# A planned single-core decoder trunk: sample keys earlier, sample state later, other weight buffers, another estimate of transfers

## The chip, the cores and the metric

The kernel runs on one core of one Trainium2 chip. The metric is the device time of one execution in microseconds (us); less is better. TensorE (PE) multiplies, with its weight loads (PEld) as a row of their own; VectorE is DVE, ScalarE is ACT, GpSimd is POOL, and SyncE (SP) issues all DMAs of this kernel from one queue. TensorE writes to PSUM; the other tiles lie in SBUF. Where this text says bank, it means a PSUM tile of 128 x 512 fp32.

## The reference, cut to what matters

One inference step of a hybrid decoder trunk (one layer). There are two groups of tokens: a **prompt** of 512 new tokens, and a **sample** group of 8 running sequences with one new token each, which bring a recurrent state and 256 useful rows of cached keys and values per sequence.

```
h = x @ w_in                                   # 1024 -> 3600
qa, ka, va, za, ga, qb, kb, vb, gb = split(h)
mixer A (4 heads): S_t = diag(a_t) S_{t-1} + k_t^T v_t;  o_t = q_t S_t     # gated linear attention
mixer B (8 heads): dilated sliding-window attention with a relative-position bias
mix = concat(o_a * silu(ga), o_b * silu(gb))
y   = mix @ w_out
x_new = layer_norm(sqrt(sqrt(2)) * x + y) * ln_g + ln_b     # alpha = 2 ** 0.25
```

Outputs are x_new for both groups, the recurrent state of both groups after the step, and the new rows of keys and values. For the sample group the state update is elementwise: state (8 sequences x 4 heads x 64 x 128, 1 MB) times a decay, plus the outer product of the new key with the new value.

## The kernel before, in words

**Dense work.** The projections are done in groups of 128 or 256 columns of w_in: ka, qa, qb, kb, vb, gb, va, ga, in this order, then w_out. A 32-bit product is made of three products of a high and a low part, so each weight tile is loaded raw (512 KB, buffers with the tag `r`, of which there are 2), copied to a high part by ACT (`hi_...`) and subtracted to a low part by DVE (`lo_...`); the two parts take buffers with the tag `w` (6) or others named below. A dense matmul has 128 weights and 256 or 264 columns. `feature` (L626) makes one group of 128 columns: two banks (u = 0 and 1, half of the tokens each), 24 matmuls for each bank, then an evacuation by another engine. `gates` (L685) calls it for the four groups of ga and of gb; their evacuation takes sigmoid steps on ACT (`sg`) and a product on DVE. The output product has two parts, `out_first` (banks `ps_yf`, transposed back as `ps_yt`) and `out_unit` (banks `ps_y`); after them come layer norm and the stores of the rows, in `norm` (L1593).

**The order is planned, not written.** All of this is made of generators (tasks), added with a priority (a low number is urgent): `add(sample_state(), 47)` (L1636), the dense chain with 100. While the program is built, a planner (`Plan`, L195) takes the next instruction again and again: of all tasks that can go on, the one whose instruction would start first by the planner's own estimate of time, ties by priority. Each engine's queue then runs in the order in which the planner emitted it; nothing is reordered on the chip. So a changed estimate in `Op` (L82) or in `issue` (L344) moves instructions on all engines. The estimate of a DMA is a rate from the shape of its rows (L105), a constant `LATE` (L76) if the queue is still busy, and a factor for DMAs that start early (L361). `At(mark, n)` holds a task until n marks of that name were emitted; `Need(tag, ...)` takes a buffer or bank from a pool and holds the task until one is free. The pools are `SLOTS` (L63: `g` 24, `w` 6, `r` 2, `sv` 5, `pt` 4, ...) and `BANKS` (L72: `d` 3, `s` 3, `t` 2). All instructions that the planner emits carry the line L366 in the profile, the one line that calls the engine; they are told apart by their tiles.

**All DMAs are issued by SP, in order.** A DMA whose buffer is not yet free holds all later ones. Eight semaphores are used in turn, so that a DMA also waits for the one that was issued eight places before it.

**The sample group**, which runs beside the prompt's dense work:
- `sample_queries` (L1209): the query rows (`q_rows`) go to a scratch row in memory (`qsd`), are broadcast back for each sequence (`qbc`, 256 KB) and multiplied on POOL with the sequence's cached keys (`past`, 512 KB, tag `sv`), four products of 128 x 256 for each of 8 sequences; DVE reduces them into `lt`.
- `sample_softmax` (L1229) turns the logits by TensorE (`ps_sl`), takes the softmax and stores it to scratch (`psd_s`). `sample_values` (L1282) broadcasts it back (`pb`, two DMAs of 256 KB for each sequence), loads cached values (`vv`, 512 KB, tag `sv`), multiplies on POOL and reduces on DVE (`o_pv`).
- `sample_state` (L1345): for each of two halves a load of the state (`s`, 512 KB), two broadcasts of the new values (`v`, 256 KB each), then eight products on ACT and eight multiply-adds on DVE of 128 x 128, and the store of the half. Its tiles have the tag `sv`, and its end sets the mark `sample`, as the end of `sample_softmax` does.

**Attention of the prompt.** For each head and query tile, scores come by `ps_s`; DVE adds a strip of bias (`strip<-tabr`, 128 KB or 256 KB, read from a table in scratch) and makes `pr`; ACT and DVE normalize it by the sums `ms`; TensorE transposes it (`ps_pt`), and ACT or DVE evacuates that as `pt`.

**Weights' buffers.** `Group.part` (L482) takes a buffer for a high or low part: tag `w`, and for w_out alone also `sv` (once the mark `sample` stands at 2, which is when `sample_softmax` and `sample_state` are both through), `pt` (once the mark `ob1` stands at 4) and `g`. `first_loads` (L546) issues the first loads in a fixed order, constants (`cf`, `rb_raw`, `cm_w`, `gn`, `ct_raw`) among them, ahead of the weights' own task. `residual` (L1483) loads the rows of x that are added to the output product (`y`, 512 KB); for the third and fourth of four tiles it waits for the mark `y0_done` at 4.

## Time and profile before

| what | value |
|---|---|
| median of 3 runs | 285.9 us (285.61 to 286.2) |
| profiled execution | 285.7 us, its span 283.9 us |
| mean granted TensorE clock | 0.992 |
| HBM read, written | 46.24 MB, 6.03 MB |

The span reaches from the first to the last recorded instruction or transfer; 1.8 us of the profiled execution lie around it. The views used below are the page (busy time of each engine, slices, chain that ended last), windows (busy time of each engine in a stretch), waits (what ended an engine's idle time), the chain in order of time (start, length, what), and groups by line and tile. Busy time of PE is modelled: a matmul is shown longer than the time until the next one starts, so that back-to-back matmuls overlap in the record.

### The profile page before, as it was taken

What the parts mean: (1) busy time and instruction counts of PE and PEld (TensorE: products, weight loads), DVE (VectorE), ACT (ScalarE), POOL (GpSimd) and SP (SyncE); (2) the same over time, 40 slices, a digit from 0 to 9 for tenths busy, and PEclk for the clock granted to TensorE, in tenths of its full rate; (3) what the DMA queues carried; (4) which work ended last, traced back from release to release, by engine and by line L of the source; (5) the groups of instructions that cost most, each with busy time, mean ns of one, the idle gap of its engine ahead of it and who ended that gap; (6) DMA issues with size and microseconds to landing.
All of it is one profiled execution on the core that took longest, in us unless ns stands there. A gap on an engine that the chain in (4) does not pass through costs nothing.

```text
span 283.9 us, 7064 instructions
## 1 busy us (share of the span) xinstructions
PE 272.5 (96%) x2760; PEld 253.3 (89%) x2760; DVE 208.4 (73%) x499; ACT 157.8 (56%) x450; POOL 54.5 (19%) x72
## 2 busy tenths in 40 slices
PE   8999999999999999999999899999999999999990
PEld 5899999998999999988989899999999999997880
DVE  3846797997969976579778896336679797439855
ACT  5738654543655755378868663426589886213201
POOL 4000000000295039300034354443000000000000
PEclk9999999999999999999999999999999999999996
DMA  6965622276874698747999999988455994872311
GB/s 197 290 179 174 182 76 76 76 204 156 302 207 141 175 279 254 205 150 227 233 209 199 214 231 234 221 215 182 121 166 160 260 284 146 209 138 111 131 76 74
DMA packets 59945, 52.27 MB, mean 184 GB/s; under 512 B 12507, under 2 KB 50693, under 8 KB 59911
## 3 DMA queue, kind: packets, MB, share of 16 engines
q1 hardware_dynamic: 59802, 51.73, 68.9%
q8 instruction: 22, 0.36, 0.5%
q14 instruction: 13, 0.10, 0.1%
q10 hardware_dynamic: 108, 0.07, 0.1%
HBM read 46.24 MB, written 6.03 MB: 184 GB/s over the span
## 4 chain that ended last, share of the span: by engine, by line
PE 72%; DMA 12%; DVE 8%; ACT 4%; issue 2%; SPq 1%; DVEq 0%; ACTq 0%
PE ps_qb L366 8%; PE ps_y L366 8%; PE ps_yf L366 7%; DMA strip<-tabr 7%; PE ps_gb L366 5%; PE ps_qa L366 4%; PE ps_vb_f L366 4%; PE ps_va_f L366 4%; PE ps_va L366 4%; PE ps_vb L366 4%; PE ps_ga L366 4%; PE ps_kb L366 3%; PE ps_ka L366 3%; DMA s<-in_state_dram 3%; DMA x_raw<-in_xT_dram 2%; PE ps_pt L366 2%
## 5 line engine op out<-in xcount | busy, mean ns | idle before, releaser
L366 POOL TENSOR_TENSOR past<-past,qbc 128x256 f32<-128x256 f32 x32 | 25.3, 825 | 90.5 <-DMA past<-in_ck_dram 88.6
L366 POOL TENSOR_TENSOR vv<-vv,pb 128x256 f32<-128x256 f32 x32 | 26.0, 844 | 48.9 <-DVE gb L366 24.4
L366 ACT ACTIVATE pr<-pr,ms 128x128 f32<-128x128 f32 (+3 forms) x45 | 24.4, 549 | 14.9 <-DVE ms L366 14.8
L366 DVE CUSTOM_DVE_ANT_0 pr<-ps_s,strip 128x128 f32<-128x128 f32 (+3 forms) x32 | 14.4, 481 | 3.3 <-DMA strip<-tabr 2.0
L366 PE MATMUL ps_pt<-cf,pr 128*128 128x128 f32 x80 | 14.0, 276 | 0.3 <-DVE pr L366 0.2
L366 ACT ACTIVATE sg<-sg 128x264 f32<-128x264 f32 (+1 forms) x32 | 13.9, 433 | 0.3
L366 PE MATMUL ps_ka<-xx,hi_ka 128*128 128x264 f32 (+1 forms) x64 | 13.2, 303 | 0.7 <-DVE xx L366 0.7
L366 ACT COPY pt<-ps_pt 128x256 f32<-128x256 f32 (+3 forms) x27 | 11.4, 431 | 4.3 <-PE ps_pt L366 4.1
L366 PEld LDWEIGHTS ps_ka<-xx,hi_ka 128*128 128x128 f32 x64 | 10.8, 201 | 1.7 <-DVE xx L366 1.1
L366 DVE TENSOR_REDUCE o_pv<-vv 128x4 f32<-128x1024 f32 x8 | 9.7, 1214 | 1.6 <-POOL vv L366 1.6
L366 PEld LDWEIGHTS ps_pt<-cf,pr 128*128 128x128 f32 x80 | 9.4, 140 | 1.4 <-issue 0.5
L366 DVE TENSOR_SCALAR pr<-pr,ms 128x512 f32<-128x512 f32 (+3 forms) x19 | 10.0, 528 | 0.4
L366 ACT ACTIVATE rstd<-mv 128x1 f32<-128x1 f32 x4 | 0.7, 203 | 16.6 <-DVE mv L366 16.6
L366 ACT COPY feat_y<-ps_yf 128x256 f32<-128x256 f32 x8 | 3.0, 373 | 12.0 <-PE ps_yf L366 12.0
L366 PE MATMUL ps_pv<-pt,v 128*64 128x256 f32 (+1 forms) x96 | 9.5, 348 | 0.0
L366 DVE TENSOR_REDUCE lt<-past 128x16 f32<-128x1024 f32 x8 | 9.5, 1201 | 0.0
L366 PE MATMUL ps_ka<-xx,lo_ka 128*128 128x264 f32 (+1 forms) x32 | 9.3, 290 | 0.0
L366 PEld LDWEIGHTS ps_pv<-pt,v 128*64 128x64 f32 x96 | 6.3, 137 | 2.9
L366 DVE TENSOR_TENSOR xx<-x_raw,xx 128x520 fp32r<-128x520 f32 (+2 forms) x9 | 5.7, 640 | 4.1 <-ACT xx L366 4.1
L366 ACT ACTIVATE d<-d 128x512 f32<-128x512 f32 x11 | 6.8, 644 | 3.4 <-DVE d L366 3.4
L366 PE MATMUL ps_s<-kp,qh 64*128 64x128 f32 (+3 forms) x64 | 8.4, 345 | 0.0
L366 DVE COPY_PREDICATED near<-cm,ps_l 128x256 f32<-128x256 uint8 x12 | 6.1, 541 | 2.3 <-PE ps_l L366 2.3
(532 smaller groups left out, 1031.6 us busy)
## 6 DMA issues: line engine op xcount, KB each, us to landing
past<-in_ck_dram SPq DMA_DIRECT2D x8, 512.0 KB
vv<-in_cv_dram SPq DMA_DIRECT2D x8, 512.0 KB
pb<-psd_s SPq DMA_DIRECT2D x16, 256.0 KB
s<-in_state_dram SPq DMA_DIRECT2D x4, 512.0 KB
qbc<-qsd SPq DMA_DIRECT2D x8, 256.0 KB
strip<-tabr SPq DMA_DIRECT2D x8, 256.0 KB
y<-in_xp_dram SPq DMA_DIRECT2D x4, 512.0 KB
x_raw<-in_xT_dram SPq DMA_DIRECT2D x7, 260.0 KB
```

What stands on the lines that cost most here:

```text
L366: getattr(eng.eng, op.fn)(*op.args, **op.kw)
```

## The change

Seven edits; the arithmetic is the same.

1. **Estimate of transfers.** `LATE` 600 becomes 1600, the table of rates is another, and the factor 0.8 for early DMAs is gone. The planner's order follows from these numbers.
2. **Buffers for weights.** Once `ob1` stands at 4, every weight group (not only w_out) may take `pt` buffers, and `sv` buffers once `sample_softmax` is through (mark `sample` at 1, since `sample_state` sets it no more); `g` stays for w_out.
3. **First loads.** The constants become a task `constant_loads` that starts after the first raw weight load was emitted.
4. **`feature` is cut into halves**; for ga, groups 0 and 1 are made together (half u = 0 of both, then u = 1 of both), then groups 2 and 3.
5. **Sample's keys.** The first three key loads are emitted once the first group of qb is under way, not behind the query rows.
6. **Sample's state.** The task waits for the mark `y3` too, takes `g` buffers, emits the loads of both halves before any product, has priority 16.5 instead of 47, and sets no mark.
7. **`residual`** waits for `y0_done` at 1 instead of 4.

```diff
-LATE = 600.0
+LATE = 1600.0
...
-            rate = 60 if run <= 128 else 175 if x.ap[0][1] <= 64 else 340 if run >= 4096 else 230
+            rate = 150 if run <= 128 else 225 if x.ap[0][1] <= 64 else 320 if run >= 2048 else 290 if run >= 1024 else 262
             self.xfer = max(4 * total(x) / rate, 200)
-            self.late = 600 * (rate == 175)
+            self.late = 600 * (rate == 225)
...
-            self.dma = max(self.dma, start + 1300) + op.xfer * (1.0 if start < 2700 else .8 if start < 9000 else 1)
+            self.dma = max(self.dma, start + 1300) + op.xfer
...
             tags = ("w",)
-            if self.src is w_out:
-
-                tags += ("sv",) * (plan.marks["sample"] == 2) + ("pt",) * (plan.marks["ob1"] == 4) + ("g",)
+            if plan.marks["ob1"] == 4:
+
+                tags += ("sv",) * (plan.marks["sample"] == 1) + ("pt",) + ("g",) * (self.src is w_out)
...
         yield D.dma_start(zw[:, :, :16], za)
         mark("zw")
+        add(weight_loads(), 3)
+        add(constant_loads(), 3.5)
+
+    def constant_loads():
+        yield At("raw", 1)
         yield D.dma_start(cf, c_f[:, :C_E2])
-        add(weight_loads(), 3)
...
+        for u in range(2):
+            yield from half(g, evac, u)
+        g.done(0)
+
+    def half(g, evac, u):
         yield At(g.name)
-        for u in range(2):
-            ps = yield bank("d", f"ps_{g.name}{u}")
-            for k in range(KT):
-                yield from three(ps[:, :TW[u]], k, halves(k, u, g))
-            add(evac(ps, u), 2)
-        g.done(0)
+        ps = yield bank("d", f"ps_{g.name}{u}")
+        for k in range(KT):
+            yield from three(ps[:, :TW[u]], k, halves(k, u, g))
+        add(evac(ps, u), 2)
...
-        for i in range(4):
-            yield from feature(groups[f"{n}{i}"], gate_into(n, own, i))
+        for i in ((0, 1), (2, 3)) if n == "ga" else ((0,), (1,), (2,), (3,)):
+            for u in range(2):
+                for j in i:
+                    yield from half(groups[f"{n}{j}"], gate_into(n, own, j), u)
+            for j in i:
+                groups[f"{n}{j}"].done(0)
...
     def sample_queries():
+        def keys(bi):
+            past.append((yield Need("sv", f"past{bi}", [P, 2, 512])))
+            yield D.dma_start(past[bi], ck[bi])
+
+        past = []
+        yield At("qb", 1)
+        for bi in range(3):
+            yield from keys(bi)
         yield At("qb", 8)
...
-            past = yield Need("sv", f"past{bi}", [P, 2, 512])
-            yield D.dma_start(past, ck[bi])
-            add(sample_logit(bi, past, qbc), 50)
+            if bi > 2:
+                yield from keys(bi)
+            add(sample_logit(bi, past[bi], qbc), 50)
...
     def sample_state():
         yield At("vat_out")
+        yield At("y3")
+        sv = []
         for i in range(2):
-            s4 = yield Need("sv", f"s5{i}", [P, 4, 2, P])
+            s4 = yield Need("g", f"s5{i}", [P, 4, 2, P])
...
-            v4 = yield Need("sv", f"v4{i}", [P, 4, 2, P])
+            v4 = yield Need("g", f"v4{i}", [P, 4, 2, P])
...
+            sv.append((s4, v4))
+        for i, (s4, v4) in enumerate(sv):
             for bb in range(4):
...
-        mark("sample")
...
         if t in (2, 3):
-            yield At("y0_done", 4)
+            yield At("y0_done", 1)
...
-    add(sample_state(), 47)
+    add(sample_state(), 16.5)
```

## The prediction

> **What bounds the kernel now.** I read the page first, for the busy shares and the chain that ended last.

> ```profile
> PE 272.5 (96%) x2760; PEld 253.3 (89%) x2760; DVE 208.4 (73%) x499; ACT 157.8 (56%) x450; POOL 54.5 (19%) x72
> ...
> PE 72%; DMA 12%; DVE 8%; ACT 4%; issue 2%; SPq 1%; DVEq 0%; ACTq 0%
> ...
> L366 PE MATMUL ps_ka<-xx,lo_ka 128*128 128x264 f32 (+1 forms) x32 | 9.3, 290 | 0.0
> ```

> TensorE is the bound: every other engine has a quarter of the span or more to spare, and the rest of the chain is made of places where PE waited. The change leaves the number of dense matmuls alone, so it can save only PE's idle time. Windows of ten to fifty us show where that lies (window, its length, then busy us of PE, PEld, DVE, ACT and POOL).

> ```profile
> 0.00:10.00 10.00, 8.12 (x35) 5.46 (x36) 4.92 (x13) 5.71 (x10) 3.18 (x8) 1.00 0.77 238
> ...
> 60.00:80.00 20.00, 19.30 (x294) 17.75 (x295) 17.61 (x41) 10.34 (x29) 4.03 (x5) 1.00 0.77 226
> ...
> 90.00:100.00 10.00, 9.95 (x86) 9.47 (x86) 9.76 (x28) 6.51 (x23) 0.99 (x1) 1.00 0.60 176
> 150.00:160.00 10.00, 9.36 (x76) 8.42 (x75) 8.49 (x20) 7.07 (x20) 3.38 (x4) 1.00 0.99 208
> 160.00:170.00 10.00, 9.75 (x83) 9.21 (x85) 9.61 (x21) 7.89 (x20) 6.93 (x8) 1.00 0.99 225
> 220.00:230.00 10.00, 9.80 (x139) 9.39 (x136) 7.77 (x28) 8.92 (x39) 0.00 (x0) 1.00 1.06 262
> 240.00:250.00 10.00, 9.82 (x82) 9.60 (x81) 5.58 (x17) 2.22 (x7) 0.00 (x0) 1.00 0.86 198
> 270.00:284.00 14.00, 6.39 (x52) 6.04 (x50) 7.05 (x14) 1.40 (x6) 0.00 (x0) 0.83 0.19 76
> ```

> All other windows show PE full. Between 10 and 270 us PE is idle for 0.70 + 0.05 + 0.64 + 0.25 + 0.20 + 0.18 = 2.02 us; the rest is the start (1.88) and the end (7.61). A dense matmul starts every 0.12 us (the row of x84 below: 10.27 / 84) and is shown with 0.29 us (the row of `lo_ka`), so each stop costs 0.17 us more than its idle time. With eight stops (three in 60 to 80, two in 150 to 170, one in each of the others) that is 2.0 + 1.4, about 3.4 us: **the most that the middle can give back**. The waits of PE and the chain name the causes.

> ```profile
> PE ps_gb L366 <- DVE ms L366: 0.9, 1, 0.9
> PE ps_ka L366 <- DVE xx L366: 0.7, 2, 0.3
> PE ps_l L366 <- issue: 0.4, 1, 0.4
> PE ps_pt L366 <- DVE pr L366: 0.2, 1, 0.2
> PE ps_yf L366 <- DVE ga L366: 0.2, 1, 0.2
> PE ps_yf L366 <- DVE lo_wo__3663 L366: 0.2, 1, 0.2
> ```

> ```profile
> 22.93 10.27 PE ps_qa L366 x84
> ...
> 142.09 15.15 DMA strip<-tabr
> ...
> 158.56 1.13 DVE o_pv L366
> ...
> 160.25 1.81 PE ps_gb L366 x13
> ```

> The largest stop is at 160 us: gb's next bank is freed by a DVE product that stands behind the last head's softmax, and this waited for a bias strip that took 15.15 us from issue to landing.

> **The change, part by part.** (a) *Keys early, and the sample's chain.* POOL waits for keys from the start:

> ```profile
> POOL past L366 <- DMA past<-in_ck_dram: 88.6, 4, 72.3
> ```

> ```profile
> 36.00:58.00 22.00, 22.00 (x406) 21.62 (x406) 20.10 (x38) 11.35 (x22) 0.00 (x0) 1.00 0.27 74
> 120.00:128.00 8.00, 8.00 (x71) 6.83 (x68) 6.02 (x20) 5.81 (x16) 0.00 (x0) 1.00 0.41 133
> 128.00:157.00 29.00, 29.00 (x244) 25.92 (x243) 22.92 (x61) 22.88 (x56) 6.48 (x8) 1.00 0.99 218
> ```

> In the new order three key loads (3 x 512 KB) stand right behind the first load of kb, so they run in the stretch from 36 us with the DMA engines at 0.27, and cost nothing there: at 218 GB/s (the row of 128 to 157) they take 7 us of 22 that are three quarters free. They are no longer among the strips and query broadcasts around 70 us, so POOL can start at about 71 instead of 76 us (72.3 of wait behind its first work). Its remaining waits for keys, 88.6 - 72.3 = 16.3 us, shrink; I estimate that the last key product comes 6 to 8 us earlier. All that hangs on it moves alike: the sample's softmax, its store, and the 8 value loads and 16 broadcasts that fill the stretch from 128 us at 0.99. They start while the engines are at 0.41 (120 to 128). The strip issued at about 141 us then has some 8 us less queue ahead of it. It needs to land only 1.2 us sooner for the stop to vanish: idle 0.64 + 0.25, and twice 0.17 hidden, **-1.2 us**. The next thing late there would be DVE's `o_pv` behind POOL's values, which move forward with the chain.

> (b) *60 to 100 us.* Idle 0.75 and four stops' 0.17, 1.4 in all. The 0.4 of "issue" with its 0.17 is PE's own and stays. The others are waits for DVE, which is 88% busy in 60 to 80 and 98% in 90 to 100 us. The strips land sooner without keys beside them, but POOL now works beside DVE from 71 us. I bound it between all of it gone (-0.8) and the opposite (+0.8), and take **-0.3**. The same product shows why I don't take more: a low part of 128 x 1024 on DVE, without POOL and beside it.

> ```profile
> L366 DVE TENSOR_TENSOR lo_kb__982<-raw_kb__768,hi_kb__981 128x1024 fp32r<-128x1024 f32 x1 | 1.2, 1225 | 0.1
> L366 DVE TENSOR_TENSOR lo_kb__1198<-raw_kb__926,hi_kb__1197 128x1024 fp32r<-128x1024 f32 x1 | 1.8, 1766 | 0.0
> ```

> It grew by 0.54 us. [...]

> (c) *State late.* Sixteen multiply-adds on DVE and as many products on ACT leave the stretch of 207 to 238 us, as do 2 MB of loads and broadcasts and 1 MB of stores.

> ```profile
> L366 DVE SCALAR_TENSOR_TENSOR s<-v,ka_s,s x16: 341/344/352, 208.2 to 237.7; 128x128 f32<-128x128 f32 x16
> L366 ACT ACTIVATE s<-s,a_s x15: 385/394/470, 207.7 to 237.2; 128x128 f32<-128x128 f32 x15
> ```

> That frees 16 x 0.344 = 5.5 us on DVE and 16 x 0.394 = 6.3 us on ACT. With it the last w_out weights, which waited for `r` and other buffers, are split earlier (in the new order all their splits stand ahead of the mixing of A's output), so the stop of 240 to 250 goes: 0.18 + 0.17, **-0.35**. The stop of 220 to 230 (0.20 + 0.17) is a bank held until DVE evacuates a gate; it has less in front of it, but interleaved gates put the last evacuation as close to the bank's next use as before. I take half, **-0.18**; bounds -0.37 and +0.4.

> Where the work goes: behind `y3`, between the output's evacuations. DVE waits there today.

> ```profile
> DVE lt L366 <- ACT feat_y L366: 7.1, 3, 3.1
> DVE y L366 <- PE ps_y L366: 3.3, 2, 1.9
> DVE y L366 <- PE ps_yt L366: 1.9, 2, 1.5
> ```

> In the new order the first half's eight multiply-adds (2.75 us) and four of the second stand ahead of the row tiles, into waits of 7.1 + 1.9 us; the last four (1.4 us) go among the layer norm, with 3.3 us of waiting for PE left. So **0** at the end, with one condition: the vectors must have landed (first rival). ACT has 1.40 us of work in the last 14.

> (d) *Gates by halves, more buffers, constants as a task, residual at 1.* Two of ga's groups alternate by bank; each bank still takes 24 matmuls, 2.9 us, and its evacuation has two other banks' time, so 0; without that cover a bank waits for an evacuation as in the 0.20 row. More buffers let `va` and `ga` weights be split earlier: 0, as PE waits for none of them today. The constants behind the first weight load: the start's waits are for x (0.7, `xx`), whose loads come first in both orders: 0, bounds -0.3 and +0.3. The two `y` loads come earlier, in front of nothing that PE waits for: 0.

> (e) *The new order itself.* Some forty of the joints between PE and other engines have moved, by up to forty-five dense matmuls, when the two orders are laid side by side. Each may be a new stop, none of which the trace of before can show. Bounds: 0, and two stops of the size of the largest today, 2 x (0.9 + 0.17) = 2.1. I take one like the `issue` row, **+0.4**, since the six that exist are mostly this size.

> Sum: -1.2 - 0.3 - 0.35 - 0.18 + 0.4 = -1.6 us, on the profiled 285.7 (span 283.9 and 1.8 around it): 284.1. The profiled execution lies 0.2 below the median of 285.9, so 284.3 by the median.

> The end itself stays: after the last matmul comes a chain of one tile's layer norm and its store.

> ```profile
> 262.66 13.74 PE ps_y L366 x82
> 276.42 0.43 DVE y L366
> ```

> From 276.42 to the span's end of 283.9 it is 7.5 us that the diff doesn't touch.

> **The rivals.** *The state comes too late (slower).* DVE runs in order, so from the first multiply-add of the second half on, all row tiles stand behind that half's vectors. Their broadcasts are issued behind eight stores of key rows, each of which waits for the landing of an earlier DMA, and the load of the second half waits for A's output (`mla`) to be mixed, which TensorE first takes at 234.9 us. The rows say when these things are wanted, and what the state's own load can take:

> ```profile
> L366 PE MATMUL ps_yf<-mla,hi_wo__3249 x8: 282/286/287, 234.9 to 240.1; 128*128 128x264 f32 x8
> ```

> ```profile
> L366 DVE SCALAR_TENSOR_TENSOR y<-y,ps_yt x8: 403/415/422, 240.1 to 255.8; 128x256 f32<-128x256 f32 x8
> ```

> ```profile
> 219.31 7.24 DMA s<-in_state_dram
> ```

> If load and broadcasts each took 7.24 us with the stores between, from 236 on, the vectors would land near 251 us; DVE wants them some 2 us (four multiply-adds and more) ahead of the last `y` additions, which run up to 255.8 and will come 1.6 sooner, so at about 252: nothing. If the broadcasts took as long as the strip's 15.15 us, they would land near 259 us, DVE would stand for some 6.5 us, of which 3.3 are covered by its waits for PE: +3.2, so 284.3 + 3.2, about 287.5. It decides from a landing at about 255 us. Against it: DMA share after 236 us is moderate (0.86 in 240 to 250, with the stores). [...]

> *POOL in DVE's way (no change or slightly slower).* Some five two-input DVE operations more run beside POOL between 71 and 90 us; at up to 0.54 us each DVE is 2.7 us later, and a stretch where DVE is nearly full passes up to 1.6 on: the -0.3 becomes +1.3, and the total 285.9.

> *The strip is late all the same (the change doesn't do what it says).* If the planner puts other loads, of va's weights and values, ahead of that strip, the 15.15 us stay and the -1.2 is lost: 284.3 + 1.2 = 285.5.

> **How the numbers follow.** The forecast (a gain of 0.6 to 3) 0.56; the strip late 0.12 (half of it faster, half within); POOL in the way 0.12 (a third each); the state too late, or several new stops of (e) together, 0.20 (slower). A measurement of this kernel can tell about 0.2% (0.6 us) from no change. So faster 0.56 + 0.06 + 0.04 = 0.66, within 0.06 + 0.04 = 0.10, slower 0.04 + 0.20 = 0.24. The range: below, all that the middle has goes but issue's 0.57, -2.8, and the start's -0.3 with it, so 282.8; above, 287.0, which leaves out about one in ten, a state later than 257 us.

> **What would show it.** In the profile after: POOL's first key product near 71 us; a strip that lands before 156 us and no PE wait on `ms` near 160; PE full in 240 to 250; DVE's `s` products at 245 to 262 with no wait on `v<-vad`; the last `y` evacuation some 1.5 us earlier and 7.5 us from the end. Wrong would be: PE idle between 10 and 270 us still near 2 us but at other places (e), or DVE idle before `s` near 250 us and the row tiles late.

## The result, and the profile after

The changed kernel took **289.8 us** (median of 4 executions, 289.27 to 290.6) beside 286.05 (285.61 to 286.42) of the kernel before: ratio **1.0147 [1.0104, 1.019]**, slower, where 284.3 was forecast with a range to 287.0. The profiled execution is 289.65 us with a span of 287.9, so 4.0 us more span than before. Two later comparisons of the same two kernels gave 1.0009 and 1.006 (e9 and e13 below, on two chips); all further ratios are to the kernel before on the same chip, with a 95% interval. Medians and ratios leave out executions in a slower state of the chip, from which the profiles of e6, e8, e9, e10 and e12 come, so those spans are not compared.

The page of after, busy times and the shares of the chain that ended last:

```profile
PE 272.4 (95%) x2760; PEld 253.3 (88%) x2760; DVE 207.2 (72%) x500; ACT 157.3 (55%) x449; POOL 59.9 (21%) x72
...
PE 69%; DMA 13%; DVE 12%; issue 2%; ACT 2%; SPq 0%; DVEq 0%; ACTq 0%
```

PE has the same 2760 matmuls and the same busy time (272.5 before). All of the loss is therefore PE's idle time. The windows of after that answer to those of before (window, length, busy us of PE, PEld, DVE, ACT, POOL, then clock, DMA share, GB/s):

```profile
60.00:70.00 10.00, 8.30 (x202) 7.72 (x201) 6.73 (x12) 2.92 (x5) 0.00 (x0) 1.00 0.57 156
70.00:80.00 10.00, 9.39 (x81) 8.88 (x82) 9.17 (x23) 5.82 (x19) 7.75 (x8) 1.00 0.29 92
80.00:90.00 10.00, 9.88 (x90) 9.16 (x89) 8.21 (x25) 7.42 (x26) 5.95 (x9) 1.00 0.74 217
...
110.00:120.00 10.00, 8.02 (x65) 7.04 (x64) 5.57 (x9) 4.41 (x12) 5.06 (x4) 1.00 0.36 104
...
160.00:170.00 10.00, 8.40 (x70) 8.05 (x69) 9.96 (x23) 7.18 (x19) 3.56 (x5) 1.00 0.64 177
...
220.00:230.00 10.00, 10.00 (x164) 9.63 (x157) 6.54 (x22) 8.62 (x37) 0.00 (x0) 1.00 0.62 184
...
240.00:250.00 10.00, 10.00 (x85) 10.00 (x84) 4.51 (x17) 3.92 (x12) 0.00 (x0) 1.00 0.96 213
```

Between 10 and 270 us PE is now idle for 1.70 + 0.61 + 0.12 + 1.98 + 1.60 = 6.01 us, where it was 2.02: 4.0 more, which is the whole difference of the spans (the start is the same, and the end differs by 0.1). The stops of before at 220 to 230 and 240 to 250 are gone; three others have come or grown, at 65, at 113 and in 160 to 170 us. PE's waits in after name what ended each (us in total, times, longest):

```profile
PE ps_l L366 <- issue: 1.7, 1, 1.7
PE ps_pt L366 <- DVE pt L366: 1.6, 1, 1.6
PE ps_pt L366 <- DVE pr L366: 1.6, 2, 0.9
...
PE ps_pt L366 <- ACT pr L366: 0.6, 1, 0.6
PE ps_vb_f L366 <- DVE lo_vb__1796 L366: 0.4, 1, 0.4
```

The chain of after in order of time (start, length, what):

```profile
62.11 1.80 PE ps_l L366 x113
63.91 1.70 issue
65.61 0.49 PE ps_l L366 x15
...
104.20 8.24 DMA sel<-in_c_f_dram
112.67 0.28 DVE pt L366
113.00 0.33 PE ps_pt L366
...
115.15 0.68 DVE lo_vb__1796 L366
...
145.80 13.93 DMA strip<-tabr
...
169.26 0.41 DVE pr L366
...
280.34 0.43 DVE y L366
```

**113 us.** `sel` is a table of 56 KB that `sample_softmax` loads when it needs it; it took 8.24 us from issue to landing. DVE's timeline shows who stood behind it (start, length, operation, in brackets the wait before it):

```profile
106.58 1.20 DVE L366 TENSOR_REDUCE lt<-past 128x16 f32<-128x1024 f32 x1
...
112.53 0.21 DVE L366 TENSOR_TENSOR l<-ln_new,sel 32x64 f32<-32x64 f32 x1 [4.76 <-DMA sel<-in_c_f_dram]
112.67 0.27 DVE L366 COPY pt<-ps_pt 128x128 f32<-128x128 f32 x1
```

DVE ran in order: a product of 0.21 us that the sample wants held the evacuation of `pt`, which TensorE wanted and whose bank `ps_pt` had been written by 109.74 us, and the split `lo_vb__1796` (PE's 0.4) behind it. In the kernel before the same load is issued even later, at 105.9 us, but the product stands behind the evacuations of `pt` in DVE's queue and starts at 114.8; PE lost nothing there. DVE's timeline of before:

```profile
111.48 0.41 DVE L366 COPY pt<-ps_pt 128x256 f32<-128x256 f32 x1
...
114.83 0.21 DVE L366 TENSOR_TENSOR l<-ln_new,sel 32x64 f32<-32x64 f32 x1 [0.20 <-DMA sel<-in_c_f_dram]
```

**65 us.** The stop is called `issue`: PE waited for nothing that the profile shows. It cuts the third batch of 128 small matmuls `ps_l`, after 113 of them here and after 109 in before, with 1.70 us here and 0.41 there. The chain of before:

```profile
62.75 1.75 PE ps_l L366 x109
64.50 0.41 issue
64.90 0.54 PE ps_l L366 x19
```

The page's list of queues has one of the kind `instruction`:

```profile
q8 instruction: 22, 0.36, 0.5%
```

(packets, MB, share). In the trace of after, a block of 16 KB on it began 0.88 us after the start of that batch, in before 0.19 us ahead of it. What sets its time is the question of the second group of runs (there: the instruction block).

**160 to 170 us.** The strip lands at 145.80 + 13.93 = 159.73 us (157.24 before), and the splits and `o_pv` products that waited with it fill DVE for 9.96 of the next 10 us, ahead of the `pr` that PE waits for.

**The end.** From the last `ps_y` evacuation at 280.34 us to the end of the span are 7.6 us, against 7.5.

### The profile page after: what moved, and what is told of

Read it like the earlier page. It is cut to its first block, busy times and chain, and to the rows that moved or that the text cites. A ratio compares the mean times of both kernels' runs of the same rounds, so it can differ in the third digit from the quotient of the medians.

```text
span 287.9 us, 7062 instructions
## 1 busy us (share of the span) xinstructions
PE 272.4 (95%) x2760; PEld 253.3 (88%) x2760; DVE 207.2 (72%) x500; ACT 157.3 (55%) x449; POOL 59.9 (21%) x72
## 4 chain that ended last, share of the span: by engine, by line
PE 69%; DMA 13%; DVE 12%; issue 2%; ACT 2%; SPq 0%; DVEq 0%; ACTq 0%
PE ps_ga L366 8%; PE ps_yf L366 8%; PE ps_qb L366 8%; DMA strip<-tabr 8%; PE ps_y L366 8%; PE ps_qa L366 4%; PE ps_va_f L366 4%; PE ps_va L366 4%; PE ps_ka L366 3%; DMA sel<-in_c_f_dram 3%; PE ps_gb L366 3%; DMA x_raw<-in_xT_dram 2%; PE ps_l L366 2%; PE ps_vb_f L366 2%; PE ps_vb L366 2%
## 5 line engine op out<-in xcount | busy, mean ns | idle before, releaser
L366 POOL TENSOR_TENSOR past<-past,qbc 128x256 f32<-128x256 f32 x32 | 28.1, 910 | 87.6 <-DMA qbc<-qsd 68.5
L366 POOL TENSOR_TENSOR vv<-vv,pb 128x256 f32<-128x256 f32 x32 | 28.7, 927 | 42.4 <-DMA pb<-psd_s 15.7
L366 ACT ACTIVATE pr<-pr,ms 128x128 f32<-128x128 f32 (+3 forms) x48 | 25.4, 542 | 10.0 <-DVE ms L366 9.8
L366 DVE CUSTOM_DVE_ANT_0 pr<-ps_s,strip 128x128 f32<-128x128 f32 (+3 forms) x32 | 14.5, 480 | 10.0 <-PE ps_s L366 6.2
L366 PE MATMUL ps_pt<-cf,pr 128*128 128x128 f32 x80 | 13.9, 279 | 3.9 <-DVE pt L366 1.6
L366 ACT COPY pt<-ps_pt 128x256 f32<-128x256 f32 (+3 forms) x26 | 10.7, 425 | 9.7 <-PE ps_pt L366 9.6
L366 PEld LDWEIGHTS ps_pt<-cf,pr 128*128 128x128 f32 x80 | 9.2, 140 | 5.5 <-DVE pt L366 1.8
L366 PE MATMUL ps_ka<-xx,hi_ka 128*128 128x264 f32 (+1 forms) x64 | 13.1, 302 | 0.7 <-DVE xx L366 0.7
L366 ACT ACTIVATE sg<-sg 128x264 f32<-128x264 f32 (+1 forms) x32 | 13.5, 422 | 0.4
L366 PEld LDWEIGHTS ps_ka<-xx,hi_ka 128*128 128x128 f32 x64 | 10.8, 200 | 1.5 <-DVE xx L366 1.1
L366 DVE TENSOR_REDUCE lt<-past 128x16 f32<-128x1024 f32 x8 | 9.6, 1206 | 1.3 <-POOL past L366 1.3
L366 ACT COPY feat_y<-ps_yf 128x256 f32<-128x256 f32 x8 | 3.0, 373 | 13.3 <-PE ps_yf L366 13.3
L366 DVE TENSOR_REDUCE o_pv<-vv 128x4 f32<-128x1024 f32 x8 | 9.7, 1210 | 0.0
L366 PE MATMUL ps_pv<-pt,v 128*64 128x256 f32 (+1 forms) x96 | 9.5, 348 | 0.0
L366 PE MATMUL ps_ka<-xx,lo_ka 128*128 128x264 f32 (+1 forms) x32 | 9.3, 290 | 0.0
L366 DVE TENSOR_SCALAR pr<-pr,ms 128x512 f32<-128x512 f32 (+3 forms) x16 | 8.6, 545 | 0.3
L366 PEld LDWEIGHTS ps_pv<-pt,v 128*64 128x64 f32 x96 | 6.3, 137 | 2.9
L366 PE MATMUL ps_s<-kp,qh 64*128 64x128 f32 (+3 forms) x64 | 8.3, 345 | 0.0
L366 DVE COPY lt<-ps_yf 128x8 f32<-128x8 f32 x7 | 1.2, 166 | 9.9 <-ACT feat_y L366 9.8
L366 DVE TENSOR_TENSOR xx<-x_raw,xx 128x520 fp32r<-128x520 f32 (+2 forms) x9 | 5.8, 640 | 3.4 <-ACT xx L366 3.3
L366 ACT ACTIVATE d<-d 128x512 f32<-128x512 f32 x11 | 6.6, 638 | 2.7 <-DVE d L366 2.6
L366 DVE COPY_PREDICATED near<-cm,ps_l 128x256 f32<-128x256 uint8 x12 | 6.1, 533 | 2.0 <-PE ps_l L366 2.0
```

The costliest lines, as they stand in the source:

```text
L366: getattr(eng.eng, op.fn)(*op.args, **op.kw)
```

## The experiments

Theory: the loss is PE's idle time at DVE's in-order wait for `sel` and at the instruction block, both products of the new order, not of any edit's own work. Rivals: the late state, the estimate by itself, the halves, the buffers, the early keys. Edits 3 and 7 have no run of their own.

### The wait for sel: e1, e9, e13, e14

e1 and e14 are the same kernel in two comparisons: the changed one with `sel` a constant, loaded with the others at the start.

```diff
+    sel = cst("sel", [64, C_AV - C_E2])
...
         yield D.dma_start(gn, gnorm)
+        yield D.dma_start(sel, c_f[:64, C_E2:C_AV])
...
-        sel = yield Need("t1", "sel", [64, C_AV - C_E2])
-        yield D.dma_start(sel, c_f[:64, C_E2:C_AV])
...
-        free(sel)
```

> The changed kernel, but the table sel (56 KB, wanted by DVE's l) is loaded with the constants at the start and not at 104.2 us. Theory A (the stop of PE at 113 us is DVE standing behind sel's landing, with pt and the split lo_vb behind it in DVE's order): no wait for sel, no PE stop of 1.6 and 0.4 us at 113 to 116, total 2.0 to 2.6 us less than the changed kernel, about 287.3. Rival B (DVE is late there anyway, behind the sums of the key products, and takes the time from elsewhere): the stop shrinks by less than 0.8 us and the total stays within 0.8 us of the changed kernel.

Measured: 0.9948 [0.9904, 0.9993], 286.1 us beside 287.6; profiled span 284.4. Its windows:

```profile
60.00:70.00 10.00, 8.77 (x206) 8.20 (x205) 7.18 (x13) 2.91 (x5) 0.00 (x0) 1.00 0.65 168
...
110.00:120.00 10.00, 10.00 (x83) 9.10 (x82) 8.86 (x20) 5.92 (x17) 4.03 (x4) 1.00 0.44 118
```

The stop at 113 is gone, that at 65 stays. e9 and e13 are the changed kernel unaltered, on two chips.

> The changed kernel as it is, on the chip of the next three. Theory A (the four stops are made by the order, and come in each execution): 1.0 to 1.9 per cent slower than before, the stops of PE at 65 (issue), 78, 113 and 116, and between 160 and 171 us, no stop between 220 and 250. Rival B (they are an accident of one execution): the stops at 113 and 116 are gone or the time is within 0.5 per cent of before.

Measured: 1.0009 [0.997, 1.0049], 287.5 beside 286.9. The stops at 65 (1.1 us) and 113 (1.9) are there again, but on that chip the changed kernel is level with before. Before has no profile on that chip, so why is open.

> The changed kernel, beside the next three on one chip. Theory A: the stops of PE at 65 (1.1 to 1.7 us, issue) and at 113 us (1.4 to 1.9, behind sel) come in the profile again, since they are made by the order; those of 160 to 171 vary with the landing of the last strip (0.4 to 2.7 so far), so that the total lies between level with before and 1.5 per cent slower. Rival B: the stop at 113 is below 0.8 us in a kernel that is level with before.

> The changed kernel with sel early (as e1). Theory A: without the stops of 113 and 116 us, 0.5 to 0.9 per cent (1.4 to 2.6 us) less than e13. Rival B: within 0.3 per cent of e13, since the time is lost again at the late strip.

Measured on one chip: e13 1.006 [1.0018, 1.0102], 288.5 us, span 288.0; e14 0.9971 [0.9932, 1.001], 286.0 us, span 283.8: **2.5 us** between the two by this edit. In e14 `l` still stands right ahead of that evacuation on DVE, but it starts at 105.45 us without a wait. From about 113 us on the edit also gives another order, so later stops differ too. The windows of e13, and then those of e14:

```profile
60.00:70.00 10.00, 9.04 (x207) 8.36 (x205) 7.22 (x14) 3.23 (x7) 0.00 (x0) 1.00 0.62 171
...
110.00:120.00 10.00, 7.71 (x52) 7.34 (x53) 5.62 (x9) 3.78 (x11) 5.06 (x4) 0.83 0.34 92
```

```profile
60.00:70.00 10.00, 10.00 (x219) 9.35 (x219) 8.40 (x16) 3.78 (x9) 0.00 (x0) 1.00 0.73 205
...
110.00:120.00 10.00, 10.00 (x82) 9.09 (x82) 6.74 (x16) 3.92 (x14) 4.00 (x4) 1.00 0.42 115
```

In e13 the granted clock was 0.83 in the window of the stop, with 52 matmuls in 7.71 busy us, where after, at 1.00, has 65 in 8.02. e14 had no `issue` stop, though its order up to there and its state loads are those of e1, which had one of 1.23 us; its instruction block began 1.03 us ahead of the batch. So this stop came in one execution of the same kernel and not in another.

### The instruction block: e5, e15, e11, e18, e12

Two loads of 512 KB of the old state (`s40`, `s41`) stand right before the third batch, at 56.47 us. These kernels move them to 41 to 44 us; e5 is that on top of e1.

```diff
     def sample_past():
...
+        yield At("qb", 3)
+        s4s = []
+        for i in range(2):
+            s4s.append((yield Need("sv", f"s4{i}", [P, 4, 2, P])))
+            yield D.dma_start(s4s[i].rearrange("p b m v -> p (b m) v"), ...)
...
-        s4s = []
-        for i in range(2):
-            s4s.append((yield Need("sv", f"s4{i}", [P, 4, 2, P])))
-            yield D.dma_start(s4s[i].rearrange("p b m v -> p (b m) v"), ...)
```

> The kernel of e1 (changed, sel early), and the two loads of the sample's old state that DVE and PE use at 66 us (512 KB each, issued at 56.6 and 57.9 us there) are issued once the third group of qb is under way, near 43 us. Theory A (PE's stop of issue at 65 us is its 16 KB block of instructions, read at 62.6 to 63.8 us, behind and beside those two loads): the stop of 1.2 us falls below 0.5, the span is 0.7 to 1.2 us below e1's 284.4. Rival B (the stop is where the block's border falls among the 128 short matmuls, whatever DMA does): it stays at 1.0 or more, the span within 0.3 us of e1's.

Measured: 0.9928 [0.9891, 0.9965], 284.8 us beside 287.1; span 283.0, 1.4 less than e1's on another chip. The two intervals overlap; what the profiles show is the stop. One window of after, and the same of e5:

```profile
64.00:65.60 1.60, 0.00 (x0) 0.00 (x0) 0.11 (x1) 0.00 (x0) 0.00 (x0) 1.00 0.32 53
```

```profile
64.00:65.60 1.60, 1.60 (x58) 1.24 (x51) 1.54 (x4) 0.26 (x1) 0.00 (x0) 1.00 0.23 29
```

PE runs through. e15 is the same move in the changed kernel, with `sel` left as it was:

> The changed kernel with the old state's two loads early and sel late as it was. Theory A: the stop of issue at 65 us goes (1.1 to 1.7 us), and with DVE's l behind the evacuation of pt in this order sel's landing costs PE less than 0.8 us: 0.6 to 1.2 per cent less than e13. Rival B: 0.3 per cent or less.

Measured: 0.9993 [0.9945, 1.0041], 0.7% below e13 on the same chip; span 284.1, no `issue` stop. The order of DVE's queue changed too: DVE still waits 2.4 us for `sel`, at 105 us, but nothing that PE wants stands behind it. e11 is the move in the kernel before, e18 the move and the early keys in it.

> The kernel before with the two loads of the sample's old state (used at 66 us) once the third group of qb is under way. Theory A (PE's block of instructions waits beside these loads in the order of before too): PE's stop of issue at 65 us (0.4) is gone, the rest as before within 0.5 us: 0.3 to 1.0 us less than before. Rival B: the stop stays, or another comes where the buffers of the later keys are freed otherwise: within 0.3 us or slower.

> The kernel before with early keys (e16) and the old state's loads early (e11). Theory A (the two gains are of different stops, issue at 65 and the late strip at 160, and add up): no stop over 0.5 us at 65 or 160, 1.0 to 2.0 per cent faster than before. Rival B (five buffers are held by keys and state at once, and the later keys come late): new stops of 1 us or more between 75 and 170 us, under 0.5 per cent faster.

Measured: e11 **0.9831 [0.9774, 0.9887]**, 283.1 us, span 283.0; e18 0.9904 [0.9871, 0.9937], 283.8 us, span 282.5. Neither has an `issue` stop. The gains were not seen to add up: e18, on another chip, gains less than e11, which has six executions. e12 has all three cures in the changed kernel, a second table (`cts`) early, and copied by ACT instead of DVE, among them:

```diff
+    def late_table():
+        yield At("qb", 1)
+        raw = yield Need("pr", "cts_raw", [66, T_W - T_D])
+        yield D.dma_start(raw, c_t[:, T_D:])
+        yield S.copy(cts, raw)
+        free(raw)
+        mark("cts")
```

> The changed kernel with both small tables of the sample's softmax (sel, 56 KB, and cts, 67 KB) loaded early and the old state's loads early (as e5). Theory A (small tables that land late in front of DVE's queue and the state beside PE's instructions are the change's loss): no stop of PE over 0.5 us between 60 and 130 us, 0.5 to 1.2 per cent faster than before, the span 282 to 283.5. Rival B (the late strip and the split of va's weights set the rest, and move about with each order): stops of 1 to 3 us together remain between 155 and 190 us, and the span is 283.5 to 286.

Measured: 0.9891 [0.9848, 0.9933]. No stop above 0.3 us is left between 60 and 130 us; stops of 0.6 and 1.5 us stay at 160 and 162 us, though the strip lands at 155.5 us there, sooner than in before.

### The parts alone: e2, e3, e4, e7, e8, e17

e2 puts the late state into the kernel before (edit 6 with its priority 16.5 and the buffers it needs); e3 puts the estimate there (edit 1 alone):

```diff
-LATE = 600.0
+LATE = 1600.0
...
-            rate = 60 if run <= 128 else 175 if x.ap[0][1] <= 64 else 340 if run >= 4096 else 230
+            rate = 150 if run <= 128 else 225 if x.ap[0][1] <= 64 else 320 if run >= 2048 else 290 if run >= 1024 else 262
...
-            self.dma = max(self.dma, start + 1300) + op.xfer * (1.0 if start < 2700 else .8 if start < 9000 else 1)
+            self.dma = max(self.dma, start + 1300) + op.xfer
```

> The kernel before with the sample's state late alone (waits for y3, g buffers, both loads ahead, priority 16.5, and weights of w_out may take sv buffers at mark sample = 1). Theory A (this part does what it should: the stops at 229 and 242 us go and the end is untouched): 0.5 to 0.8 us less than before, about 285.4. Rival B (what the part gains is lost again in DVE's order behind the state's vectors or at the end): within 0.3 us of before or slower.

Measured: 1.0049 [1.0013, 1.0085]. The stops that before has at 229 and 242 us are gone, but `oa` comes late at 234 us, and PE stands for 2.2 us. The windows of e2 show the stop and the clock behind it:

```profile
233.00:234.00 1.00, 0.00 (x0) 0.00 (x0) 0.90 (x5) 0.00 (x0) 0.00 (x0) 1.00 0.94 351
234.00:235.00 1.00, 0.29 (x1) 0.29 (x2) 0.93 (x5) 0.95 (x3) 0.00 (x0) 0.79 1.12 335
235.00:236.00 1.00, 1.00 (x6) 1.00 (x6) 1.00 (x2) 0.44 (x1) 0.00 (x0) 0.50 0.94 174
...
237.00:238.00 1.00, 1.00 (x7) 1.00 (x6) 0.49 (x2) 0.00 (x0) 0.00 (x0) 0.51 0.85 135
238.00:239.00 1.00, 1.00 (x10) 1.00 (x10) 0.51 (x2) 0.46 (x1) 0.00 (x0) 1.00 0.30 41
```

> The kernel before with the new estimate of transfers alone (LATE and the rates). Theory A (the loss of the change comes from the order that the new estimate makes together with the early keys; alone it moves DVE's l ahead of the evacuation of pt less): up to 2 us slower than before, 286 to 288, with the stops of PE between 60 and 170 us. Rival B (the estimate alone carries the loss): 3 us or more slower, 289 or above.

Measured: **1.0359 [1.0306, 1.0412]**, span 295.5, with PE's longest wait

```profile
PE ps_yf L366 <- ACT oa L366: 4.8, 1, 4.8
```

The new rates by themselves, on the old tasks, make the worst order of all. The chain leads to this stop through ACT's and DVE's split of a weight of w_out that landed at 238.6 us and stands ahead of what `oa` needs. At 114 us PE loses 1.1 us, because `pt` stands on DVE behind `cts`, another small table that comes by DMA (4.69 us from issue to landing). e17 is the reverse: the changed kernel with the old rates.

> The changed kernel with the estimate of transfers as before (LATE 600, the old rates). Its order up to 165 us is that of e16. Theory A (the new estimate made the order that loses, the other parts gain): 0.3 to 1.2 per cent faster than before, no stop of PE over 1 us between 70 and 170 us, but the stop of issue at 65 may stay (0.4 to 1.0). Rival B (the other parts lose by themselves at the end, as in e2): level with before or slower, with a stop of 1 us or more between 160 and 245 us.

Measured: 0.9942 [0.9905, 0.9978], 285.0 us, span 283.5. `sel` is asked for earlier (102.4 us), DVE does not wait for it, and the 113 stop is gone; 0.35 us of idle time are left between 70 and 240 us. The stop at 65 stays, with 1.45 us, so the estimate is not what makes that one. The other edits together gain; the estimate turns that into a loss. e4 takes the early keys out of the changed kernel (`yield At("qb", 1)` and its three loads), e7 the halves of ga, e8 the extra buffers:

```diff
-        for i in ((0, 1), (2, 3)) if n == "ga" else ((0,), (1,), (2,), (3,)):
+        for i in ((0,), (1,), (2,), (3,)):
```

```diff
-            if plan.marks["ob1"] == 4:
+            if self.src is w_out:
 
-                tags += ("sv",) * (plan.marks["sample"] == 1) + ("pt",) + ("g",) * (self.src is w_out)
+                tags += ("sv",) * (plan.marks["sample"] == 1) + ("pt",) * (plan.marks["ob1"] == 4) + ("g",)
```

> The changed kernel with the first three key loads back behind the query rows. Its order up to 190 us is that of the new estimate alone. Theory A (early keys are a part of the loss: POOL beside DVE from 72 us, and sel caught between more loads): 1 us or more less than the changed kernel, below 288.8. Rival B (the early keys gain, and the estimate loses): 0.5 us or more above the changed kernel.

> The changed kernel with ga's four groups made one after the other, as before. Its order up to 190 us is the changed kernel's. Theory A (the halves are a matter of the end only, and there they keep the last gate's evacuation and oa off PE's way): a stop of PE of 1 to 3 us appears between 220 and 245 us, as in e2. Rival B (the halves do nothing): no such stop, the time within 0.3 us of the changed kernel.

> The changed kernel with pt and sv buffers for w_out's weights alone, as before. Theory A (the buffers let w_out's parts be split earlier, and without them the stop of PE of 2.2 us that e2 showed at 234 us comes): a stop of 1 to 3 us between 220 and 245 us. Rival B (with the state late the buffers are not needed): no such stop, the time within 0.3 us of the changed kernel.

Measured: e4 1.0064 [1.0026, 1.0103], e7 1.0047 [1.0007, 1.0086], e8 1.01 [1.0055, 1.0146]. All three stay slower than before, so no one of these parts carries the loss. Each order is another one, and each has stops of 1 us and more in 60 to 190 us (e7: 1.5 at 65, 1.4 at 113). Without the halves 220 to 250 us stays full, so the halves do nothing that can be seen; without the buffers 0.7 us comes back at 239 us, where w_out's splits are late.

### Keys and strips: e16, e10, e6

e16 is the kernel before with the early keys alone, e10 is e1 without them, e6 is e1 with a fourth strip buffer.

```diff
+        yield At("qb", 1)
+        for bi in range(3):
+            yield from keys(bi)
...
+            if bi > 2:
+                yield from keys(bi)
```

```diff
-    t2=3, st=3,
+    t2=3, st=4,
```

> The kernel before with the first three key loads early alone. Theory A (the prediction's step a: the sample's chain and with it the last strip move forward): the stop of 160 us goes or halves, 0.2 to 0.6 per cent less than before. Rival B (the keys fill the queue so that the small tables or PE's instructions come late): new stops of 1 us or more between 60 and 130 us, level with before or slower.

Measured: 0.996 [0.9928, 0.9992], 285.3 us, span 282.6. The windows of e16:

```profile
150.00:160.00 10.00, 10.00 (x86) 9.78 (x86) 8.83 (x23) 8.75 (x22) 1.27 (x3) 1.00 0.96 189
160.00:170.00 10.00, 10.00 (x86) 9.64 (x83) 8.41 (x25) 8.33 (x23) 5.12 (x8) 1.00 1.11 209
```

The stop near 160 is gone and the strip lands at 155.5 us. But the softmax's store goes out at 128.23 us, as before (128.03): what the prediction gave as the reason, an earlier chain, is not what happened. One load stands between the earlier strips and this one in SP's queue, where there were four transfers; whether that is all of it is open.

> The changed kernel with sel early (as e1) and the key loads back behind the query rows. Theory A (early keys hurt through sel's landing alone): with sel early they help or do nothing, so this kernel is level with e1 or up to 1.5 us slower, PE's stops between 70 and 120 us under 1 us in both. Rival B (POOL beside DVE from 72 us costs PE time by itself): this kernel is 0.5 us or more below e1's 284.4 span, without the stops of 78 and 80 us.

Measured: 1.0005 [0.9961, 1.0048], where e1 had 0.9948 and e14, the same kernel, 0.9971. The chips differ and the intervals overlap, so whether the early keys help once `sel` is out of the way is not shown.

> The kernel of e1 with four buffers for strips of bias instead of three, so that the last three strips stand ahead of more of the value loads and broadcasts in SP's queue. Theory A (the stops of PE at 159 and 168 us are the last head's strip, 13 to 15 us in a queue filled by the values): the last strip lands at least 3 us sooner, the stops (0.5 + 1.3) fall below 0.5 together, the span is 1.2 to 1.8 us below e1's 284.4. Rival B (DVE is full there, 9.9 of 10 us, and late with strip or without): the stops stay at 1.2 or more.

Measured: 1.0122 [1.0075, 1.017], and the strip lands at 157.0 instead of e1's 156.1 us: so a fourth buffer does not bring it sooner. Instead a new order has a new stop, at the next table. PE's wait in e6:

```profile
PE ps_vb_f L366 <- DVE lo_vb__1797 L366: 4.2, 1, 4.2
```

and DVE's timeline of e6:

```profile
118.17 0.59 DVE L366 CAST cts<-cts_raw 66x258 fp32r<-66x258 f32 x1 [3.10 <-DMA cts_raw<-in_c_t_dram]
```

The same mechanism as with `sel`, with another small table, in a kernel where `sel` was cured.

## Why the prediction was wrong

**(e) The new order itself, +0.4: failed, by size.** One stop like the `issue` row was taken for all new joints, with two stops of the largest kind as the upper bound (2.1). One new joint alone, DVE's `l` one place ahead of the `pt` evacuation, made 1.98 us of idle PE in 110 to 120 us, and curing it gave back 2.5 us (e13 to e14). The clue stood in the two orders: a DVE instruction that waits for a DMA had moved ahead of one that PE waits for. The prediction asked what stands behind DVE's wait for the state's vectors; it did not ask it of `sel`. That the estimate makes this order is shown by the runs together. Of the six profiles with the old rates (before, e2, e11, e16, e17, e18) none has a stop of PE between 100 and 130 us. Of the eight with the new rates and `sel` loaded late, seven have stops there behind `sel` or `cts`, 0.6 to 2.3 us in each; only e15 has none.

**(b) 60 to 100 us, -0.3: wrong sign.** Idle went from 0.75 to 2.43 us. The largest part, 0.41 to 1.70, is the row that the prediction set aside as "PE's own". It is not: in all 20 profiles the stop goes by the start of the 16 KB block on the queue q8. There is none where the block began 1.0 us or more ahead of the batch (e14, and 1.9 us or more in e5, e11, e12, e15, e18). There are 0.4 to 0.8 us where it began up to 0.2 us ahead (before, e2, e16), and 1.0 to 1.7 where it began after the batch, by up to 0.9 us (the other eleven). The five kernels without the state loads there are the five with the earliest blocks. But e14 had no stop either with the loads in place, so what is shown is that moving the loads removes the stop, not that they alone make it. Nor does the new estimate: e16 and e17, with the old rates, have 0.82 and 1.45. The idle time in 70 to 100 us grew as well, 0.35 to 0.73, with POOL at work from 72 us: that is the direction of the rival *POOL in DVE's way*, at a quarter of its price. But e14, e15 and e17 start POOL as early and lose 0.11 us or less there, so POOL's start alone does not make it.

**(a) Keys early, -1.2: its reason failed in the old order, its gain in the new.** In the old order the stop went and 1.2 us were gained (e16), as forecast, but by luck, since the chain did not come earlier. In the changed kernel POOL's first wait is as forecast:

```profile
POOL past L366 <- DMA qbc<-qsd: 68.5, 1, 68.5
POOL past L366 <- DMA past<-in_ck_dram: 18.8, 4, 5.8
```

The first product starts at about 72 us. But the softmax's store came 3 us sooner (124.91), not 6 to 8, since DVE's wait for `sel` stood in that chain too (with `sel` early, in e1, it goes out at 122.18). The last strip was issued 3.7 us later than before, which is as much as PE had by then lost more than before. DVE waited 1.98 us for it, and the stops there went from 0.89 to 1.60. The rival *the strip is late all the same* has come true in this profile, and at more than its price. But the strip alone does not make these stops. In e14 and e15 it lands at 155.9 and 155.2 us, sooner than in before, and a stop of 1.74 us stands between 156 and 168 us all the same. In e17, with the old rates, it lands at 160.8, and 0.29 us are lost. What sets them in the new order is open.

**(c) State late, -0.53 of stops: right.** 220 to 250 us is full, and no row of DVE's waits names the state's vectors. That rival, which carried most of the chance for slower, did not come, but it was near: in the profiles of e9 (the same kernel), e12 and e15 DVE waits 1.7 to 2.4 us for these vectors, without a stop of PE behind it. In the old order the same edit costs (e2), since `oa` is late there.

**(d) 0: right for the halves** (e7). The buffers are worth more than 0 in the new order, some 0.7 us of idle PE in the one profile without them (e8). The constants and `residual` were not tried alone, but the start of after is as idle as that of before (8.12 us busy in the first ten). **The end, 0: right** (7.6 us).

The total: idle -0.38 at (c), +1.68 at (b), +0.71 at (a), +1.98 at (e), 3.99 in sum, against the span's 4.0. The mechanism is shown for the stop at 113, and in part for that at 65; for 160 to 170 us it is open, and so is the size of the whole. In the three comparisons of the changed kernel it came to 1.5%, 0.1% and 0.6%, each with the stops at 65 (1.70, 1.1 and 1.0 us) and 113 (1.6, 1.9 and 2.3). Their lengths differ from one execution to the next, but that alone does not explain a time level with before in e9. The kernel before moves as well, with medians of 286.1 to 287.6 in the different comparisons, and e11 lies in a narrow 282.3 to 284.9. Why e11 gains 1.7% when before's profile shows only some 0.6 us at 65 us stays open.

## What to carry to other kernels

Where an order is planned, look in the new order of each in-order engine for instructions that wait for a DMA, however small, and ask which instruction that the bounding engine needs now stands behind each; a new joint can cost what a DMA takes from issue to landing, here 8.24 us (`sel`) and 13.93 (the strip), less its lead, and not what an average stop costs today. Load small tables at the start (2.5 us here, e13 to e14). Another estimate of single transfers, meant to be better, need not make a better order: here it lost 3.6% by itself, and the changed kernel without it gained 0.6%, the size that was forecast for the whole.

## What the runs showed of the hardware

**A stop of 1.45 us was followed by half the clock, one of 1.70 was not.** In e2 above, a stop of 2.2 us is followed by three microseconds at 0.50 or 0.51, with 6 or 7 matmuls in each instead of 10. In e17 a shorter one, of 1.45 us, is followed by the same, as its windows show:

```profile
64.00:65.00 1.00, 0.03 (x1) 0.00 (x0) 0.21 (x1) 0.00 (x0) 0.00 (x0) 1.00 0.03 7
65.00:66.00 1.00, 0.52 (x17) 0.46 (x16) 0.00 (x0) 0.00 (x0) 0.00 (x0) 0.83 0.85 176
66.00:67.00 1.00, 1.00 (x7) 1.00 (x6) 0.95 (x2) 0.26 (x1) 0.00 (x0) 0.50 0.94 334
...
68.00:69.00 1.00, 1.00 (x6) 1.00 (x6) 1.00 (x2) 0.98 (x1) 0.00 (x0) 0.50 0.14 40
```

The stop of 1.70 us in after left the clock at 1.00 (its windows of 60 to 70 us above). No run shows what decides it.

**POOL's long products ran beside DVE's.** POOL's key product takes 910 ns in the mean in after, 825 in before. The page's row and the row of its tile, with the least, the median and the longest of the 32 in ns:

```profile
L366 POOL TENSOR_TENSOR past<-past,qbc 128x256 f32<-128x256 f32 x32 | 28.1, 910 | 87.6 <-DMA qbc<-qsd 68.5
...
L366 POOL TENSOR_TENSOR past<-past,qbc x32: 717/740/1994, 72.3 to 118.7; 128x256 f32<-128x256 f32 x32
```

The eight products of after that took more than 1 us (1.06 to 1.99) each ran beside a product or a difference of two SBUF tiles on DVE (`kd`, `qa`, `lo_...`). The other 24 took 0.72 to 0.79 us, with none of these beside them but for 0.23 us of a `lo_kb` in one. In before five took 1.19 to 1.72 us, each beside a `lo_...`; but four with 0.57 to 0.69 us of one beside them took 0.73 to 0.79.
